# Hybrid encoder trunk on one core: the squared-ReLU units evicted wider and unscaled, one Strassen product's bank kept through all groups, PSUM divided into pairs

## The chip, the cores and the metric

The kernel runs on one core of a Trainium2 chip. The metric is the device time of one launch in microseconds: the median of three runs, with the lowest and the highest.

## The reference, cut to what matters

Two layers act on 256 tokens of width 2048. Each has three groups of attention heads with one input and one output projection, and then a squared-ReLU MLP with 8192 hidden units:

```python
def rmsnorm(x, g):
    xf = x.astype(jnp.float32)
    y = xf * lax.rsqrt(jnp.mean(xf * xf, axis=-1, keepdims=True) + EPS)
    return (y * g.astype(jnp.float32)).astype(x.dtype)
...
    for l in range(DEPTH):
        h = rmsnorm(x, norm_mix[l])
        proj = jnp.einsum('bsd,de->bse', h, w_in[l])
        ...
        mix = jnp.concatenate([rmsnorm(oa, out_gain_a[l]),
                               rmsnorm(ob, out_gain_b[l]),
                               rmsnorm(oc, out_gain_c[l])], axis=-1)
        x = x + jnp.einsum('bse,ed->bsd', mix, w_o[l])
        h = rmsnorm(x, norm_mlp[l])
        u = jax.nn.relu(jnp.einsum('bsd,df->bsf', h, w_up[l]))
        x = x + jnp.einsum('bsf,fd->bsd', u * u, w_down[l])
    return rmsnorm(x, norm_final)
```

The row factor of the MLP's norm, r = 1/sqrt(mean(x^2) + eps), is one number for each token. Since relu(r z)^2 = r^2 relu(z)^2 for r > 0, it can be applied to z, to the squared unit, or to what the down projection adds to x.

## The kernel before, in words

**Steps.** Every weight matrix streams through the core once. The work is a list of `Step`s, each with one weight tile of 512 KB. `load` (L1012) issues its DMA seven steps ahead; `split` (L1026) makes two fp32r halves of it two or three steps ahead, the high half with a cast on ScalarE (L1036, tile `whi`) and the rest with a subtraction on VectorE (L1037, tile `wlo`), three buffers of each. Then the step's `mm` runs on TensorE. Activations are held as two halves likewise, so that a product takes three matmuls: high by high, high by low, low by high.

**The background queue.** What is not a weight step (transposes, attention scores, probabilities, small sums) is a piece in a queue; `tick` after each step emits pieces whose delay is over, within a budget. That gives the order in the program. The framework then schedules each engine's instructions ahead of time by priority and readiness, so the order on an engine is fixed when the chip runs but is not the program's.

**PSUM, eight banks of 512 numbers a partition.** `score_banks` is a tile of two banks (tag S, one buffer): attention scores, and in the MLP the accumulators `a` and `d` of Strassen's products. The other six are one pool of single banks (tag `bank`), which `mm_bank` (a product's accumulator, two for each product) and `tr_bank` share: `tr_bank` serves transposes of operands (L223, L255, L271), of probabilities (L380, two banks a unit), probabilities times values (L392, L399), group sums (L443) and the row of reciprocals (L505).

**The MLP.** A layer has 32 up units q of 256 hidden columns, four steps each: z is made transposed, hidden columns on partitions, tokens in the free dimension; L675 gives 512 columns (256 of high, 256 of low activations), L680 adds the low weights. The unit's `evac` folds the two 256 column halves together in two banks (ScalarE copy L653, VectorE add L654, twice), multiplies max(z, 0) by the token's r from `rrow`, a tile with the 256 factors in every partition (L655), squares (L658), splits into halves (`u`, L660 and L661), forms Strassen's four sums S1 to S4 (`sums_of`, L696 to L698) and splits those (L700, L701). `rrow` is made by `rows` in `mlp_rs`: a diagonal of r on VectorE, a matmul by ones into a `tr_bank`, a copy. Unit 0's eviction is put off until after step (1, 0), because `rrow` is needed for it.

The down projection goes in eight groups of four units. `strassen_steps` computes 2 x 2 blocks (two token blocks, two column blocks of 512) with seven products, P1 to P7 (L806): P2 accumulates in a bank `b` of its own, P1, P6, P5 and P3 one after the other in `a`, P7 and P4 in `d`. After a product its bank is added to or subtracted from x (`evac`, L777). The first six groups have a second such set (pair 1) over half of the units for the last two column blocks; there P2 and P4 are not evicted, but `down_steps` with `shared` goes on in `b` and `d` and evicts both (L728). Groups 6 and 7 do those columns as plain products. An order written out by hand interleaves a group's Strassen steps with the next group's up steps. `layer_end` starts the next layer's operand transposes, or the final norm.

Of the kernel before, what the change touches and what calls it, by code (L numbers as in the profile page):

```python
# [23 lines left out]
P = 128  # L24
# [19 lines left out]
def tile_trunk(ctx: ExitStack, tc: tile.TileContext, x_in, xt_in, w_in, w_o, w_up, w_down,  # L44
# [57 lines left out]
    rrow = cp.tile([P, 256], F32, name="rrow")  # L102
# [99 lines left out]
    def operand_pair(key, gcol, i, src, hT):  # L202
# [8 lines left out]
        for kk in range(2):  # L211
            nc.vector.scalar_tensor_tensor(hh[:, 1, kk, :], src[kk], gs[kk], f(hh[:, 0, kk, :]),
                                           op0=ALU.mult, op1=ALU.subtract)

# [201 lines left out]
    def mix_prep(l, grp, blk, raw, mixT, sqacc, done):  # L416
# [11 lines left out]
        if first:  # L428
            acc = sp.tile([P, 256], F32, tag="sqacc", bufs=3, name=nm("sqacc"))
# [32 lines left out]
    def mode_b(banks, h_tile, wh, wl, sub, first, last, n=512, blocks=(0, 1), lo_last=False,  # L462
               by_block=False):

        def one(t, i, part):
            kk = sub[i]
            a = h_tile[i][:, int(part == "lh"), kk, t * P:(t + 1) * P]
# [17 lines left out]

    state = {}

    def layer_steps(l):
# [6 lines left out]
        def mlp_rs():  # L495
            r = rsqrt(mean_eps(st["ss2"], 4, 1.0 / D), 2)

            def rows():

                dg = mid(F32, 2, P)  # L500
                for t in range(NT):
                    nc.vector.tensor_scalar(dg[:, t, :], ident, r[:, t:t + 1], None, op0=ALU.mult)
                ps = tr_bank()
                for t in range(NT):
                    nc.tensor.matmul(ps[:, t * P:(t + 1) * P], full, dg[:, t, :], start=True, stop=True)  # L505
# [81 lines left out]
        for name in IN_CHUNKS:  # L587
# [5 lines left out]
            for k in range(nst):  # L593
# [6 lines left out]
                def mm(wh, wl, k=k, nk=nk, nst=nst, n=n, box=box, name=name):  # L600
                    if k == 0:
                        box["b"] = [mm_bank(), mm_bank()]
                    hts = [halves(st["hT"][(k * nk + i) // 2]) for i in range(nk)]
# [9 lines left out]
        for grp in OUT_ORDER:  # L613
            blks = GROUP_BLOCKS[grp]
            for j in range(4):
                box = {}
                for bi, blk in enumerate(blks):
# [6 lines left out]
                    def mm(wh, wl, grp=grp, j=j, bi=bi, blk=blk, nb=len(blks), box=box):  # L624
                        if bi == 0:
                            box["b"] = [mm_bank(), mm_bank()]
                        mode_b(box["b"], [st["mixT"][blk]] * 2, wh, wl, [0, 1], bi == 0, bi == nb - 1)
# [12 lines left out]
        uT, sT = {}, {}  # L640

        def up_steps(g):

            out_, evacs = [], []
            for q in range(4 * g, 4 * g + 4):
                box = {}

                def evac(q=q, box=box):
                    need(("rrow", l))
                    a = mid(F32, 2, 256)  # L650
                    for i in range(2):

                        nc.scalar.copy(a[:, i, :], box["b"][i][:, 256:512])  # L653
                        nc.vector.tensor_add(a[:, i, :], a[:, i, :], box["b"][i][:, 0:256])  # L654
                    nc.vector.scalar_tensor_tensor(  # L655
                        a, a, 0.0, rrow.rearrange("p (o c) -> p o c", o=1).to_broadcast([P, 2, 256]),
                        op0=ALU.max, op1=ALU.mult)
                    nc.scalar.activation(a, a, AF.Square, bias=zero1[:, 0:1])  # L658
                    u = big(F32R, 2, 2, 256)
                    nc.scalar.copy(u[:, 0], a)  # L660
                    nc.vector.tensor_sub(u[:, 1], a, f(u[:, 0]))  # L661
                    uT[q] = u
                    sums_of(q, a)

                for s in range(4):
# [3 lines left out]
                    def mm(wh, wl, s=s, q=q, box=box, evac=evac):  # L669
                        if s == 0:  # L670
                            box["b"] = [mm_bank(), mm_bank()]
                        for kk in range(4):
                            ht = st["hT2"][2 * s + kk // 2][:, kk % 2, :]
                            for fs in range(2):
                                nc.tensor.matmul(box["b"][fs], wh[:, kk, fs * P:(fs + 1) * P], ht,  # L675
                                                 start=s == 0 and kk == 0, stop=False, skip_group_check=True)
                        for kk in range(4):
                            ht = st["hT2"][2 * s + kk // 2][:, kk % 2, :]
                            for fs in range(2):
                                nc.tensor.matmul(box["b"][fs][:, 0:256], wl[:, kk, fs * P:(fs + 1) * P], ht[:, 0:256],  # L680
# [555 lines left out]
```

## Time and profile before

| | |
|---|---|
| median of 3 runs | 1995.33 us (1994.92 to 1995.36) |
| profiled execution, span | 1993.9 us, 28351 instructions |
| TensorE busy | 1980.3 us (99%), 10134 matmul records |
| VectorE, ScalarE, GpSimd busy | 1647.0, 1247.4, 396.4 us |
| HBM | 448.65 MB read, 226 GB/s over the span |
| mean granted TensorE clock | 0.999 |

The profiled execution is known by its span, from its first to its last instruction; 1.4 us lie between it and the median of the runs. A fp32 matmul of the kernel may stand as more than one record. In the profile PE is TensorE's matmuls, PEld its weight loads, DVE VectorE, ACT ScalarE, POOL GpSimd; L777 is line 777 of the kernel. A group of instructions is told as output<-inputs by the program's tile names, then shapes, count, busy time, mean ns of one, and the idle time of the engine before them with what ended it. In a timeline row the first two numbers are start and length in us, and xN merges N instructions in a row.

### The profile page before, as it was taken

Reading aid. Unit: us, or ns where it says so; the run is one execution under the profiler, and the core shown is the slowest. Engines: PE = TensorE matmul, PEld = TensorE weight load, DVE = VectorE, ACT = ScalarE, POOL = GpSimd, SP = SyncE. Lnnn points to the kernel's source line nnn. Section 1 sums busy time; section 2 is a strip of 40 time slices with the busy share of each in tenths; the row PEclk is TensorE's granted clock in tenths of the full one; section 3 lists DMA queues with packets and bytes.
Section 4 is the critical chain, followed back from the end, with each engine's and each line's share of the span. In section 5 each row is a group of like instructions: output and inputs, shape, how many; then the busy total and the mean of one; then the engine's idle time right before and its main releaser. Section 6 shows DMA issues by size and latency. Waiting matters only on the chain.

```text
span 1993.9 us, 28351 instructions
## 1 busy us (share of the span) xinstructions
PE 1980.3 (99%) x10134; PEld 1683.2 (84%) x10134; DVE 1647.0 (83%) x2197; ACT 1247.4 (63%) x1778; POOL 396.4 (20%) x462
## 2 busy tenths in 40 slices
PE   9999999999999999999999999999999999999998
PEld 7888888888888888888888888888888888888887
DVE  6777877888888888888857678778988988888887
ACT  7667756666565656566656677566666656656664
POOL 0674620001010010100008745201010001101000
PEclk9999999999999999999999999999999999999999
DMA  9755755888888888978666467568898988989884
GB/s 341 212 164 153 235 168 190 224 260 260 252 256 243 273 248 251 273 224 252 207 190 201 153 177 222 169 190 251 233 273 243 269 248 247 265 252 260 238 264 126
DMA packets 128635, 456.31 MB, mean 229 GB/s; under 512 B 14660, under 2 KB 16964, under 8 KB 128493
## 3 DMA queue, kind: packets, MB, share of 16 engines
q1 hardware_dynamic: 109052, 384.18, 56.4%
q0 software_dynamic: 19008, 69.21, 20.1%
q8 instruction: 80, 1.31, 0.3%
q10 hardware_dynamic: 432, 1.10, 0.1%
q14 instruction: 63, 0.51, 0.1%
HBM read 448.65 MB, written 2.11 MB: 226 GB/s over the span
## 4 chain that ended last, share of the span: by engine, by line
PE 96%; DVE 1%; DMA 1%; ACT 1%; issue 1%; SPq 0%; POOL 0%; POOLq 0%; DVEq 0%; ACTq 0%
PE mm L468 32%; PE mm L675 23%; PE S L806 18%; PE mm L680 12%; PE mm L806 3%; PE S L468 2%; PE tr L380 1%; PE tr L399 1%; DMA wraw<-in_w_in_dram 1%; PE S L343 1%; PE S L342 1%; PE tr L223 1%; DVE wlo L1037 0%; ACT big L360 0%; PE tr L392 0%
## 5 line engine op out<-in xcount | busy, mean ns | idle before, releaser
L1037 DVE TENSOR_TENSOR wlo<-wraw,whi 128x1024 fp32r<-128x1024 f32 (+1 forms) x517 | 634.3, 1233 | 200.9 <-ACT whi L1036 191.4
L1036 ACT CAST whi<-wraw 128x1024 fp32r<-128x1024 f32 (+1 forms) x517 | 541.2, 1051 | 360.2 <-PE mm L675 100.2
L675 PE MATMUL mm<-big,whi 128*128 128x512 f32 x2048 | 514.1, 390 | 0.0
L468 PE MATMUL mm<-whi,big 128*128 128x512 f32 (+1 forms) x1692 | 500.1, 384 | 0.8 <-ACT whi L1036 0.8
L675 PEld LDWEIGHTS mm<-big,whi 128*128 128x128 f32 x2048 | 380.5, 188 | 79.4 <-ACT whi L1036 2.2
L468 PEld LDWEIGHTS mm<-whi,big 128*128 128x128 f32 x1692 | 314.3, 188 | 61.8 <-ACT whi L1036 1.9
L680 PEld LDWEIGHTS mm<-big,wlo 128*128 128x128 f32 x2048 | 280.9, 190 | 21.2
L468 PE MATMUL mm<-wlo,big 128*128 128x512 f32 (+1 forms) x846 | 293.3, 382 | 0.0
L806 PE MATMUL S<-whi,big 128*128 128x512 f32 x1056 | 290.1, 396 | 0.0
L680 PE MATMUL mm<-big,wlo 128*128 128x256 f32 x2048 | 287.3, 282 | 0.0
L806 PEld LDWEIGHTS S<-whi,big 128*128 128x128 f32 x1056 | 184.3, 189 | 34.2 <-DVE x L777 2.8
L468 PEld LDWEIGHTS mm<-wlo,big 128*128 128x128 f32 x846 | 159.3, 188 | 28.7
L806 PE MATMUL S<-wlo,big 128*128 128x512 f32 x528 | 163.4, 391 | 0.0
L1036 ACT CAST whi<-side 128x1024 fp32r<-128x1024 f32 x88 | 92.5, 1051 | 85.3 <-PE mm L675 76.6
L1036 ACT CAST whi<-big 128x1024 fp32r<-128x1024 f32 x88 | 92.9, 1056 | 77.5 <-DVE big L788 27.7
L468 PE MATMUL mm<-spare,big 128*128 128x512 f32 (+1 forms) x606 | 140.2, 380 | 0.0
L1037 DVE TENSOR_TENSOR wlo<-side,whi 128x1024 fp32r<-128x1024 f32 x88 | 107.7, 1224 | 35.4 <-ACT whi L1036 34.6
L792 POOL DMA_DIRECT2D spare<-in_w_down_dram x44 | 38.1, 866 | 476.2 <-DVE wlo L1037 458.4
L468 PEld LDWEIGHTS mm<-spare,big 128*128 128x128 f32 x606 | 108.9, 188 | 20.4
L1037 DVE TENSOR_TENSOR wlo<-big,whi 128x1024 fp32r<-128x1024 f32 x88 | 107.7, 1224 | 21.5 <-ACT whi L1036 21.3
L792 POOL DMA_DIRECT2D side<-in_w_down_dram x44 | 38.3, 881 | 400.9 <-DVE mid L654 150.8
L806 PEld LDWEIGHTS S<-wlo,big 128*128 128x128 f32 x528 | 99.2, 188 | 22.2
(163 smaller groups left out, 2310.3 us busy)
## 6 DMA issues: line engine op xcount, KB each, us to landing
wraw<-in_w_up_dram SPq DMA_DIRECT2D x256, 512.0 KB, 4.8
wraw<-in_w_down_dram SPq DMA_DIRECT2D x124, 512.0 KB, 5.1
wraw<-in_w_in_dram SPq DMA_DIRECT2D x119, 512.0 KB, 3.7
side<-in_w_down_dram SPq DMA_DIRECT2D x88, 512.0 KB, 5.2
wraw<-in_w_o_dram SPq DMA_DIRECT2D x64, 512.0 KB, 3.7
side<-in_w_down_dram POOLq DMA_DIRECT2D x44, 512.0 KB, 7.5
spare<-in_w_down_dram SPq DMA_DIRECT2D x44, 512.0 KB, 5.9
spare<-in_w_down_dram POOLq DMA_DIRECT2D x44, 512.0 KB, 5.5
```

The costliest lines, as they stand in the source:

```text
L223: nc.tensor.transpose(psv[:, kk, t, :], x[:, t, c0:c0 + P], ident)
L342: nc.tensor.matmul(o, st, u.kh[:, kh, :], start=True, stop=False)
L343: nc.tensor.matmul(o, st, u.kl[:, kh, :], start=False, stop=True)
L380: nc.tensor.transpose(ps[:, c * P:(c + 1) * P], u.p[:, s, kb * P:(kb + 1) * P], ident)
L399: nc.tensor.matmul(ps, u.V[:, kb, u.kv, :, :], pt[:, kb, :], start=n == 0, stop=n == 3)
L468: nc.tensor.matmul(banks[t][:, 0:n], a, (wl if part == "hl" else wh)[:, i, :], start=first and i == 0 and part == "hh", stop=last and i == ...
L675: nc.tensor.matmul(box["b"][fs], wh[:, kk, fs * P:(fs + 1) * P], ht, start=s == 0 and kk == 0, stop=False, skip_group_check=True)
L680: nc.tensor.matmul(box["b"][fs][:, 0:256], wl[:, kk, fs * P:(fs + 1) * P], ht[:, 0:256], start=False, stop=s == 3 and kk == 3, skip_group_ ...
L792: nc.gpsimd.dma_start(tile, src(par, j, h).rearrange("p (k n) -> p k n", k=2), accum_op=ALU.add)
L806: nc.tensor.matmul(o, ops[i][a], w[:, i, :], skip_group_check=True, start=fresh and h == 0 and i == 0 and a == 0 and w is wh, stop=h == ti ...
L1036: last_act[0] = nc.scalar.copy(h[:, part], w[:, part]).ins
L1037: last_lo[0] = nc.vector.tensor_sub(lo[:, part], w[:, part], f(h[:, part])).ins
```

## The change

- `evac` of an up unit works on both banks at once: one copy, one add, Relu and Square on ScalarE, in a tile `wide` (8 x 128 columns, one buffer) that takes the four blocks and, from `sums_of`, the four sums; then one cast and one subtraction make both halves of up to all eight. No factor r is applied.
- r^2 (the power -1 of the mean square) and its negative are kept per token in `rsq`, and `residual` applies them where a product is added to x. `rows`, `rrow` and the putting off of unit 0 go.
- P2's bank is kept: it starts at group 0 and goes on accumulating. In the first pair it is evicted only after group 7, in the second only after the shared product of group 5.
- The six banks become two `pair` tiles of two banks (`mm_pair`, for products) and two single banks (`tr`, for all that `tr_bank` serves and for the two kept banks).
- The group sums of the attention outputs use the `wide` tile.

```diff
+    def four_k():
+        return sp.tile([P, 8, P], F32, tag="wide", bufs=1, name=nm("wide"))
...
-    def mm_bank():
-        return pp.tile([P, 512], F32, tag="bank", bufs=6, name=nm("mm"))
+    def mm_pair():
+        return pp.tile([P, 2, 512], F32, tag="pair", bufs=2, name=nm("mm"))
+    def mm_banks():
+        two = mm_pair()
+        return [two[:, 0, :], two[:, 1, :]]
     def tr_bank():
-        return pp.tile([P, 512], F32, tag="bank", bufs=6, name=nm("tr"))
+        return pp.tile([P, 512], F32, tag="tr", bufs=2, name=nm("tr"))
...
+    def residual(xs, bank, l, t, sign=1):
+        nc.vector.scalar_tensor_tensor(xs, bank, rsq[:, l, int(sign < 0), t:t + 1], xs, op0=ALU.mult, op1=ALU.add)
...
         def mlp_rs():
-            r = rsqrt(mean_eps(st["ss2"], 4, 1.0 / D), 2)
-            def rows():
-                dg = mid(F32, 2, P)
-                for t in range(NT):
-                    nc.vector.tensor_scalar(dg[:, t, :], ident, r[:, t:t + 1], None, op0=ALU.mult)
-                ps = tr_bank()
-                for t in range(NT):
-                    nc.tensor.matmul(ps[:, t * P:(t + 1) * P], full, dg[:, t, :], start=True, stop=True)
-                nc.vector.tensor_copy(rrow, ps[:, 0:256])
-                flags.add(("rrow", l))
-            add(rows, 0.45, delay=D_R, front=True)
+            ms = mean_eps(st["ss2"], 4, 1.0 / D)
+            nc.gpsimd.tensor_tensor(rsq[:, l, 0], ms, mone[:, 0:2], op=ALU.pow)
+            nc.gpsimd.tensor_scalar(rsq[:, l, 1], rsq[:, l, 0], -1.0, None, op0=ALU.mult)
...
                 def evac(q=q, box=box):
-                    need(("rrow", l))
-                    a = mid(F32, 2, 256)
-                    for i in range(2):
-                        nc.scalar.copy(a[:, i, :], box["b"][i][:, 256:512])
-                        nc.vector.tensor_add(a[:, i, :], a[:, i, :], box["b"][i][:, 0:256])
-                    nc.vector.scalar_tensor_tensor(
-                        a, a, 0.0, rrow.rearrange("p (o c) -> p o c", o=1).to_broadcast([P, 2, 256]),
-                        op0=ALU.max, op1=ALU.mult)
-                    nc.scalar.activation(a, a, AF.Square, bias=zero1[:, 0:1])
-                    u = big(F32R, 2, 2, 256)
-                    nc.scalar.copy(u[:, 0], a)
-                    nc.vector.tensor_sub(u[:, 1], a, f(u[:, 0]))
-                    uT[q] = u
-                    sums_of(q, a)
+                    au = four_k()
+                    a = au[:, 4:8, :].rearrange("p (k t) c -> p k (t c)", k=2)
+                    nc.scalar.copy(a, box["b"][:, :, 256:512])
+                    nc.vector.tensor_add(a, a, box["b"][:, :, 0:256])
+                    nc.scalar.activation(a, a, AF.Relu, bias=zero1[:, 0:1])
+                    nc.scalar.activation(au[:, 0:4, :].rearrange("p (k t) c -> p k t c", k=2)[:, :, ::-1, :],
+                                         a.rearrange("p k (t c) -> p k t c", t=2), AF.Square, bias=zero1[:, 0:1])
+                    sums_of(au)
+                    n0 = int(g < 6 and q % 4 < 2)
+                    uh, ul = big(F32R, 8, P), big(F32R, 8, P)
+                    nc.scalar.copy(uh[:, n0:8], au[:, n0:8])
+                    nc.vector.tensor_sub(ul[:, n0:8], au[:, n0:8], f(uh[:, n0:8]))
+                    uT[q] = uh, ul
...
-        def sums_of(q, a):
-            v = a.rearrange("p k (t c) -> p (k t) c", t=2)
-            sm = mid(F32, 4, P)
...
+        def sums_of(au):
+            nc.vector.tensor_sub(au[:, 4:6, :], au[:, 1:3, :], au[:, 0:1, :].to_broadcast([P, 2, P]))
+            nc.vector.scalar_tensor_tensor(au[:, 6, :], au[:, 5, :], -1.0, au[:, 1, :], op0=ALU.mult, op1=ALU.subtract)
+            nc.vector.scalar_tensor_tensor(au[:, 7, :], au[:, 6, :], -1.0, au[:, 3, :], op0=ALU.mult, op1=ALU.subtract)
...
                     def evac(t):
                         xs = x[:, t, j * 512:(j + 1) * 512]
-                        nc.vector.tensor_add(xs, xs, box["b"][t])
+                        residual(xs, box["b"][t], l, t)
...
-                    evac(0)
+                    if not shared or gs == (5,):
+                        evac(0)
                     evac(1)
...
             def evac(bank, t, j, sign):
                 xs = x[:, t, 1024 * pair + j * 512:1024 * pair + (j + 1) * 512]
-                op = nc.vector.tensor_add if sign > 0 else nc.vector.tensor_sub
-                op(xs, xs, bank)
+                residual(xs, bank, l, t, sign)
...
                         if (name, h) == ("P2", 0):
-                            box["b"] = mm_bank()
+                            if pair not in keep:
+                                keep[pair] = tr_bank()
+                            box["b"] = keep[pair]
...
-                                                 start=fresh and h == 0 and i == 0 and a == 0 and w is wh,
+                                                 start=fresh and h == 0 and i == 0 and a == 0 and w is wh and (bk != "b" or g == 0),
...
-                        if h == tiles[-1] and not (pair and name in ("P2", "P4")):
+                        if h == tiles[-1] and not (pair and name == "P4") and not (name == "P2" and (pair or g < 7)):
                             evac(o, *dst)
```

More of the change, by code (lines that the diff above doesn't have):

```diff
@@ L101, in tile_trunk @@
     nc.vector.memset(full, 1.0)
-    rrow = cp.tile([P, 256], F32, name="rrow")
+    rsq = cp.tile([P, L, 2, NT], F32, name="rsq")
     mhalf = cp.tile([P, 16], F32, name="mhalf")
@@ L428, in mix_prep @@
         if first:
-            acc = sp.tile([P, 256], F32, tag="sqacc", bufs=3, name=nm("sqacc"))
+            if not sqacc:
+                sqacc["all"] = four_k()
+            n = 2 * "ACB".index(grp)
+            acc = sqacc["all"][:, n:n + 2, :].rearrange("p a c -> p (a c)")
             sqacc[grp] = acc
@@ L484, in mode_b, with of @@
                     one(t, i, part)
+    def of(h):
+        return lambda part, kk, t: h[:, part, kk, t * P:(t + 1) * P]
     state = {}
@@ L601, in mm @@
                     if k == 0:
-                        box["b"] = [mm_bank(), mm_bank()]
-                    hts = [halves(st["hT"][(k * nk + i) // 2]) for i in range(nk)]
+                        box["b"] = mm_banks()
+                    hts = [of(halves(st["hT"][(k * nk + i) // 2])) for i in range(nk)]
                     mode_b(box["b"], hts, wh, wl, [(k * nk + i) % 2 for i in range(nk)], k == 0, k == nst - 1, n,
@@ L637, in layer_steps @@
                     steps.append(Step(src, 2, 512, pre, mm))
-        uT, sT = {}, {}
+        uT, keep = {}, {}
         def up_steps(g):
-            out_, evacs = [], []
+            out_ = []
             for q in range(4 * g, 4 * g + 4):
```

43 lines of the change are left out of this document (15 added, 28 removed).

## The prediction

> **What bounds the kernel now.** I read the page's busy times first, then the table by stages, the waits, the groups by shape, and the timeline where the change touches the order.
>
> ```profile
> PE 1980.3 (99%) x10134; PEld 1683.2 (84%) x10134; DVE 1647.0 (83%) x2197; ACT 1247.4 (63%) x1778; POOL 396.4 (20%) x462
> ```
>
> TensorE is busy for 1980.3 of 1993.9 us. By stages (columns: stretch, length, then busy time of PE, PEld, DVE, ACT, POOL, granted clock, DMA share, GB/s):
>
> ```profile
> 199.00:315.00 116.00, 114.86 (x586) 96.97 (x585) 93.53 (x147) 73.92 (x138) 43.55 (x49) 1.00 0.65 196
> 315.00:1000.00 685.00, 685.00 (x3503) 582.82 (x3502) 590.90 (x744) 422.63 (x520) 56.03 (x65) 1.00 0.83 246
> 1190.00:1306.00 116.00, 114.85 (x588) 97.09 (x587) 92.58 (x147) 74.09 (x139) 43.48 (x49) 1.00 0.64 195
> 1960.00:1994.00 34.00, 25.93 (x136) 22.00 (x134) 23.17 (x36) 14.72 (x22) 1.12 (x2) 0.93 0.26 94
> ```
>
> In the first layer's MLP (315 to 1000) PE never stops, though DVE is busy 86% of the time; the stage of attention and output projection loses 1.1 us in each layer, the tail 8.1 us. So work taken from DVE or ACT is worth only what PE waits for them. Those waits:
>
> ```profile
> ACT whi L1036 <- PE mm L675: 210.0, 182, 2.1
> ...
> PEld S L806 <- DVE x L777: 2.8, 15, 0.3
> PEld S L806 <- DVE x L728: 2.7, 10, 0.4
> ```
>
> ACT waits 210 us for PE to free weight buffers: the weight splits run ahead of PE, and that is the cover for all that the change does to ACT and DVE. PE's loader waits only 5.5 us for evictions.
>
> **The change part by part.** The rows that price it:
>
> ```profile
> L1037 DVE TENSOR_TENSOR wlo<-wraw,whi 128x1024 fp32r<-128x1024 f32 x515 | 633.0, 1235 | 200.9 <-ACT whi L1036 191.4 <-issue 7.9 <-PE tr L223 0.4
> L1036 ACT CAST whi<-wraw 128x1024 fp32r<-128x1024 f32 x515 | 540.0, 1052 | 360.2 <-PE mm L675 100.2 <-PE S L806 96.4 <-PE mm L468 75.0
> ...
> L777 DVE TENSOR_TENSOR x<-x,S 128x512 f32<-128x512 f32 x156 | 106.5, 683 | 1.3 <-PE S L806 1.1
> ...
> L654 DVE TENSOR_TENSOR mid<-mid,mm 128x256 f32<-128x256 f32 x128 | 47.8, 415 | 0.7
> L658 ACT ACTIVATE mid<-mid,zero 128x512 f32<-128x512 f32 x64 | 46.2, 722 | 15.2 <-DVE mid L655 15.2
> L655 DVE SCALAR_TENSOR_TENSOR mid<-mid,rrow 128x512 f32<-128x512 f32 x64 | 44.0, 687 | 0.7
> L701 DVE TENSOR_TENSOR big<-mid,big 128x512 fp32r<-128x512 f32 x64 | 43.9, 686 | 0.0
> L661 DVE TENSOR_TENSOR big<-mid,big 128x512 fp32r<-128x512 f32 x64 | 43.8, 685 | 0.0
> ...
> L653 ACT COPY mid<-mm 128x256 f32<-128x256 f32 x128 | 41.0, 371 | 24.6 <-PE mm L680 24.6
> L660 ACT CAST big<-mid 128x512 fp32r<-128x512 f32 x64 | 39.7, 620 | 1.7
> L700 ACT CAST big<-mid 128x512 fp32r<-128x512 f32 x64 | 39.5, 617 | 19.6 <-DVE mid L698 19.5
> ...
> L381 ACT CAST big<-tr 128x512 fp32r<-128x512 f32 x64 | 34.4, 590 | 0.6
> L633 DVE SCALAR_TENSOR_TENSOR x<-mm,sm,x 128x512 f32<-128x512 f32 x48 | 33.9, 744 | 0.2
> ...
> L696 DVE TENSOR_TENSOR mid<-mid 128x256 f32<-128x256 f32 x64 | 26.8, 419 | 0.0
> ...
> L697 DVE SCALAR_TENSOR_TENSOR mid<-mid,mid 128x128 f32<-128x128 f32 x64 | 18.4, 287 | 0.4
> L698 DVE SCALAR_TENSOR_TENSOR mid<-mid,mid 128x128 f32<-128x128 f32 x64 | 18.4, 287 | 0.3
> ...
> L505 PE MATMUL tr<-mid,full 128*128 128x128 f32 x8 | 1.2, 273 | 0.0
> ```
>
> (1) An up unit's eviction, 64 times. DVE before: 2 x 415 + 687 + 685 + 419 + 2 x 287 + 686 = 3.88 us. After: one add of 512 columns (683), the same sums (419 + 2 x 287), one subtraction of up to 1024 columns (1235) = 2.91 us; 62 us less in all. ACT before: 2 x 371 + 722 + 620 + 617 = 2.70 us; after: a copy of 512 from PSUM (590), Relu and Square (722 each), a cast of 1024 (1052) = 3.09 us, 25 us more. On the path I cost both at nothing: DVE and ACT stay ahead of PE. Without that cover the chain to a usable uT, longer by about 2 us (casts and subtraction of 1024 instead of 512, and the sums ahead of them), would count only where Strassen's P1 follows its unit directly, at the first group of each layer (later groups have two steps of the shared product between). Bounds 0 and 2 x 2 us; I take 0.3, since other ready matmuls can go first there.
>
> (2) Evictions to x. By the loops there are 233; P2 keeps its bank in 7 groups and the shared product's first half in 5, in each layer: 24 fewer, 16.4 us of DVE. The other 209 become scalar_tensor_tensor, 744 instead of 683 ns: 12.7 us back. On the path: the L728 waits are 10 in number, as are the starts of a group whose S banks wait behind a pair of evictions of which the first now goes (five a layer). One of them, and an undisturbed product after it:
>
> ```profile
> 446.35 1.75 PE L675 MATMUL mm<-big,whi 128*128 128x512 f32 x7
> 448.05 1.20 PE L806 MATMUL S<-whi,big 128*128 128x512 f32 x4
> ...
> 450.71 1.09 PE L806 MATMUL S<-whi,big 128*128 128x512 f32 x4
> ```
>
> Seven matmuls at 0.229 us would end their turn at 447.95, the product starts 0.10 later, and its four take 0.11 longer: 0.2 us, ten times, 2.2 us given to the change (bounds: nothing and the 5.5 us of both waits). Against it stands 0.061 us where PE waits on an eviction directly, and twice in the tail: +0.3 (bounds 0 and 3, if each reuse of Strassen's first bank paid it).
>
> (3) The row of reciprocals (L502 to L506): 8 PE records, 1.2 us busy with overlap, disappear from PE's stream: -1.0 us (0.9 to 1.2). In exchange POOL gets one tiny multiplication per layer. No DMA is added or moved, so SP's and POOL's transfers keep their order.
>
> (4) PSUM. Before, six banks served products and transposes together; now products have two pairs, and transposes, probabilities times values and small sums have two banks. Pairs are no problem: a product takes at least two steps and its eviction follows at once, so the pair before last is free. In the MLP no tr tile is made between the operand transposes and the last group, so holding both banks costs nothing there. Attention is the place. A tile's bank is held from its first PE instruction to its last DVE read:
>
> ```profile
> 90.65 1.03 PE L380 MATMUL tr<-ident,big 128*128 128x128 f32 x8
> ...
> 146.53 1.04 PE L255 MATMUL tr<-ident,big 128*128 128x128 f32 x8
> ...
> 150.19 1.03 PE L380 MATMUL tr<-ident,big 128*128 128x128 f32 x8
> ...
> 212.29 0.33 PE L255 MATMUL tr<-ident,big 128*128 128x128 f32 x1 [1.14 <-ACT big L517]
> ...
> 478.73 0.51 PE L680 MATMUL mm<-big,wlo 128*128 128x256 f32 x3
> 479.07 1.16 PE L806 MATMUL S<-whi,big 128*128 128x512 f32 x4
> ...
> 1296.23 1.03 PE L223 MATMUL tr<-ident,x 128*128 128x128 f32 x8
> ```
> ```profile
> 92.21 0.84 DVE L412 TENSOR_TENSOR mid<-tr,ot 64x256 f32<-64x256 f32 x2
> ...
> 154.02 2.82 DVE L262 SCALAR_TENSOR_TENSOR big<-tr,big 64x512 fp32r<-64x512 f32 x4 [3.52 <-ACT big L259]
> ...
> 478.29 0.68 DVE L777 TENSOR_TENSOR x<-x,S 128x512 f32<-128x512 f32 x1
> ...
> 1295.87 0.87 DVE L212 SCALAR_TENSOR_TENSOR big<-tr,gn,big 128x256 fp32r<-128x256 f32 x2
> ```
>
> At 146.53 two tiles are written; DVE has read the first by 154.02 + 1.41 = 155.4. At 150.2 the next two are begun, into banks that will no longer exist: the first would wait 5.2 us. Done so for 152 tiles, 42 start with two or more unread (the first in the 90.65 row, its second tile, until 93.05; the last at 1296.66, 0.07 us). Kept in today's order and shifted by what was waited already, the waits sum to 57.8 us: the upper bound. The lower is zero, since PE's order is a list schedule in which ready matmuls pass waiting ones: at 478 to 479 the product that had to wait for an eviction (ends 478.97) starts at 479.07, in the middle of an up step, at a loss of 0.1 us. Where the schedule misjudged the other engines it cost 1.14 us (212.29). I take a wait up to one projection step as bridged (the 12 matmuls of the row below, 2.75 us, 0.229 each) and the rest of longer ones as paid: per layer 5.22, 3.62 and 3.19 are longer, the rest is 2.47 + 0.87 + 0.44 = 3.8, so +7.6 us for two layers.
>
> ```profile
> 76.61 2.75 PE mm L468 x12
> ```
>
> The Trainium skill (Trainium Kernel Development and Optimization, Best Practices) says that consistent bubbles can mean that SBUF or PSUM ran out. By that every one of the 42 would leave a bubble; at the 212.29 row's 1.14 us each this part would be 48 us, an estimate, against 7.6 by the rows.
>
> **The sum**: 0.3 - 2.2 + 0.3 - 1.0 + 7.6 = +5.0 us on the span of 1993.9. The median of the runs, 1995.33, stands 1.4 above that span, so 2000.3 us.
>
> **The rivals.** *All bridged* (transfer of waits hidden anyway): the D_T, D_PV and similar delays leave room, and PE always has a projection step to run. Against it: ACT and DVE in attention run in a fixed order and stood still in cross waits, as 212.29 shows. 1995.3 - 2.6 = 1992.7 us, within 0.2%. *Faster*: with 66 us taken from DVE, all 5.5 us of eviction waits go, and the evacuations ahead of the query transposes come early enough for the 1.14 us in both layers: -1.0 - 5.5 - 2.3 = 1986.5 us; it decides from 4.0 us on and only if no bank wait is paid. *Order kept*: if PE cannot pass the waiting transposes, -2.6 + 57.8, so 2050 us; the 479.07 row speaks against it. *Clock*: the granted clock is 1.00 in the stages with a 1.1 us stop and 0.93 in the last 34 us, which hold 8.1 us of idle: 2.4 us lost. If the three long waits of each layer are paid in full (24.1 us) and the four longest each cost such a loss (9.5), 1995.3 - 2.6 + 33.6 = 2026 us. The Trainium skill (TensorE: Matmul & The Clock Gate, Part 1) has the clock halved after an idle window of about 3.4 us; by that the loss would be some 4 x 1.7 = 6.8 us instead of 9.5, an estimate. No run here shows a stop of that length inside the kernel.
>
> **How the numbers follow.** Partly bridged 0.42 (own range 1996 to 2012; 0.10 of it under 1999.3), all bridged 0.33 (0.04 of it below 1991.3), faster 0.13, order kept 0.07, clock 0.05. About 0.2% (4.0 us) is what a measurement here can tell from no change. Faster 0.13 + 0.04 = 0.17; same 0.10 + 0.29 = 0.39; slower 0.32 + 0.07 + 0.05 = 0.44. The range 1990.5 to 2016 leaves out order kept, clock and most of the faster case, about 0.2.
>
> **What would show it.** Right: PE's waits on tr tiles with a DVE or ACT releaser in 60 to 290 and 1050 to 1280, a few us per layer; PE below full in those stages and still full in the MLP; the L728 waits for S gone; DVE near 1580 us, ACT near 1270. Wrong: no tr waits in attention (then all bridged), clock below 1.00 there, or MLP stretches in which PE waits for the new eviction's chain or for its single wide buffer.

## The result and the profile after

| | before | after |
|---|---|---|
| median | 1995.34 us (1994.92 to 1995.58, 4 runs) | 2007.65 us (2006.50 to 2008.09, 4 runs) |
| ratio to before | | 1.0059 [1.0045, 1.0073] |
| profiled span | 1993.9 us | 2005.4 us |
| mean granted clock | 0.999 | 0.999 |

The change makes the kernel 12.3 us slower. That is the sign that was forecast and lies in the range of 1990.5 to 2016 us, but it is more than twice the 5.0 us of the sum. The busy row of the page of after:

```profile
PE 1986.2 (99%) x10126; PEld 1680.8 (84%) x10126; DVE 1603.6 (80%) x1975; ACT 1276.6 (64%) x1714; POOL 402.1 (20%) x464
```

VectorE has 43 us less to do, TensorE eight records fewer, and yet TensorE is "busy" 6 us longer. The ends of matmuls are modelled in this profile, so its busy time says little here; how long each stage lasts says more. The marks are the first `mm<-big,whi` matmul of a layer's first up unit and the last record of that layer's MLP in a Strassen product; each number is the distance between two such starts or ends in the trace (us):

| kernel | start to MLP 0 | MLP 0 | to MLP 1 | MLP 1 | end | span |
|---|---|---|---|---|---|---|
| before | 315.7 | 671.4 | 319.0 | 668.5 | 19.3 | 1993.9 |
| after | 321.8 | 670.9 | 323.7 | 669.1 | 19.9 | 2005.4 |
| two `tr` banks alone (e2) | 323.2 | 671.6 | 324.9 | 668.6 | 20.0 | 2008.3 |
| three `tr` banks alone (e5) | 319.7 | 672.8 | 320.3 | 671.1 | 19.3 | 2003.2 |
| kept bank alone (e3) | 315.6 | 671.4 | 318.9 | 670.0 | 19.3 | 1995.2 |
| row scaling alone (e10) | 315.1 | 669.6 | 319.0 | 667.8 | 18.6 | 1990.1 |
| new eviction alone (e4) | 314.7 | 669.7 | 319.1 | 667.8 | 18.6 | 1989.9 |
| after, six single banks (e1) | 316.3 | 669.7 | 319.1 | 667.9 | 18.6 | 1991.6 |

After against before: +6.1 and +4.7 in the two stages ahead of the MLPs, +0.1 in the two MLPs together, +0.6 at the end. TensorE's loader now waits like this (line waited for, us in total, times, longest):

```profile
PEld S L803 <- DVE x L225: 9.4, 35, 0.6
PEld tr L392 <- issue: 6.5, 14, 0.6
PEld tr L283 <- DVE big L394: 2.7, 2, 1.4
PEld tr L392 <- POOL big L383: 2.5, 2, 1.3
PEld tr L267 <- DVE avs L156: 2.0, 1, 2.0
```

L392 (L380 before) transposes probabilities, L283 and L267 operands: the `tr` tiles, with VectorE reads (L394, L156) as releasers. No wait on a `tr` tile is longer than 2.0 us. In the timeline (start, length, then idle time before it):

```profile
35.53 0.67 DVE L156 COPY avs<-tr 8x512 f32<-8x512 f32 x1
...
36.26 0.66 PE L267 MATMUL tr<-ident,big 128*128 128x128 f32 x4 [1.76 <-DVE avs L156]
```
```profile
157.65 1.84 POOL L383 TENSOR_SCALAR big<-big,sm 128x256 f32<-128x256 f32 x4
...
159.10 0.63 PE L392 MATMUL tr<-ident,big 128*128 128x128 f32 x4 [0.87 <-POOL big L383]
```

The first is a plain bank wait: the one-time product at L154 (`avp`) sits in a `tr` bank until VectorE has copied it. The second is by its releaser no bank wait: the transposes wait for probabilities that GpSimd is still scaling. The granted clock stays at 1.00 in both attention stages, and fewer matmuls fit into the same stretch (first row before, then the two of after; columns as in the prediction's table):

```profile
60.00:290.00 230.00, 228.86 (x1166) 193.51 (x1165) 179.23 (x268) 154.39 (x295) 139.88 (x160) 1.00 0.62 183
```
```profile
60.00:290.00 230.00, 226.82 (x1146) 188.59 (x1145) 176.51 (x271) 153.44 (x298) 138.62 (x159) 1.00 0.61 181
...
1050.00:1280.00 230.00, 226.77 (x1147) 188.63 (x1146) 174.16 (x268) 152.57 (x296) 137.28 (x157) 1.00 0.61 182
```

The waits of before list nothing on GpSimd at this line: there the same scaling (L371) ends at 155.94 and its transposes begin at 156.52, so nothing waits. With two banks the transposes stand in TensorE's order ahead of the scaling's end.

### The profile page after: what moved, and what is told of

It is laid out like the page before. It is cut to its first block, busy times and chain, and to the rows that moved or that the text cites. A ratio compares the mean times of both kernels' runs of the same rounds, so it can differ in the third digit from the quotient of the medians.

```text
span 2005.4 us, 28100 instructions
## 1 busy us (share of the span) xinstructions
PE 1986.2 (99%) x10126; PEld 1680.8 (84%) x10126; DVE 1603.6 (80%) x1975; ACT 1276.6 (64%) x1714; POOL 402.1 (20%) x464
## 4 chain that ended last, share of the span: by engine, by line
PE 62%; DVE 1%; ACT 1%; issue 0%; POOL 0%; POOLq 0%; DVEq 0%; ACTq 0%
PE mm L483 18%; PE mm L682 16%; PE S L803 13%; PE mm L687 8%; PE tr L803 2%; PE tr L483 1%; PE S L483 1%; PE tr L392 1%; PE tr L411 0%; PE tr L235 0%; PE S L354 0%; PE S L355 0%; DVE wlo L1034 0%; PE tr L404 0%; PE tr L267 0%
## 5 line engine op out<-in xcount | busy, mean ns | idle before, releaser
L1034 DVE TENSOR_TENSOR wlo<-wraw,whi 128x1024 fp32r<-128x1024 f32 (+1 forms) x517 | 634.1, 1233 | 220.8 <-ACT whi L1033 218.2
L483 PE MATMUL mm<-whi,big 128*128 128x512 f32 (+1 forms) x1596 | 471.7, 386 | 1.2 <-DVE x L225 0.7
L483 PEld LDWEIGHTS mm<-whi,big 128*128 128x128 f32 x1596 | 296.0, 189 | 57.7 <-ACT whi L1033 1.5
L483 PE MATMUL mm<-wlo,big 128*128 128x512 f32 (+1 forms) x798 | 279.6, 383 | 0.0
L483 PEld LDWEIGHTS mm<-wlo,big 128*128 128x128 f32 x798 | 150.5, 189 | 27.3 <-DVE wlo L1034 0.2
L1034 DVE TENSOR_TENSOR wlo<-side,whi 128x1024 fp32r<-128x1024 f32 x88 | 107.6, 1223 | 46.3 <-ACT whi L1033 46.2
L225 DVE SCALAR_TENSOR_TENSOR x<-S,rsq,x 128x512 f32<-128x512 f32 x168 | 125.5, 747 | 4.6 <-PE S L803 2.6
L1034 DVE TENSOR_TENSOR wlo<-big,whi 128x1024 fp32r<-128x1024 f32 x88 | 107.4, 1220 | 16.8 <-ACT whi L1033 16.7
```

Of the source, the lines that this page charges most:

```text
L225: nc.vector.scalar_tensor_tensor(xs, bank, rsq[:, l, int(sign < 0), t:t + 1], xs, op0=ALU.mult, op1=ALU.add)
L483: nc.tensor.matmul(banks[t][:, 0:n], a, (wl if part == "hl" else wh)[:, i, :], start=first and i == 0 and part == "hh", stop=last and i == ...
L1034: last_lo[0] = nc.vector.tensor_sub(lo[:, part], w[:, part], f(h[:, part])).ins
```

## The experiments

The theory to test: the loss is the split of the PSUM banks, and there the two that transposes share. Rivals: the new eviction (one wide buffer, a longer chain), or the kept bank that holds one of the two.

**e1: after with one pool of six single banks**, and so the copy and the add of an up unit bank by bank.

```diff
-        return pp.tile([P, 512], F32, tag="tr", bufs=2, name=nm("tr"))
+        return pp.tile([P, 512], F32, tag="bank", bufs=6, name=nm("tr"))
...
-        two = mm_pair()
-        return [two[:, 0, :], two[:, 1, :]]
+        return [pp.tile([P, 512], F32, tag="bank", bufs=6, name=nm("mm")) for _ in range(2)]
```

> The changed kernel with PSUM as before: one pool of six single banks for products and transposes, so an up unit's eviction has two copies and two adds of 256 columns instead of one of 512; the kept banks and the residual scaling stay. Bank theory (transposes have too few banks in attention): the 12 us go away, 1993 to 1996 us, and PE's waits on transposes fall back to those of the kernel before. Eviction theory (the longer chain, the single wide buffer, dearer residual additions): it stays within 3 us of the changed kernel, 2004 to 2008. Kept-bank theory (two banks fewer for the up units now hurt): slower than the changed kernel, over 2008.

Measured: 1992.84 us, 0.9986 [0.9977, 0.9995]. The whole loss is gone, and the kernel is 2.6 us faster than before. (The bank theory had 1993 to 1996.) On `tr` tiles its loader waits for the same two things as before's (3.6 us in 4 waits, 2.0 in 2) and no longer for L388, the transposes of probabilities:

```profile
PEld S L800 <- DVE x L221: 5.7, 23, 0.3
PEld tr L263 <- ACT big L522: 3.6, 4, 1.6
PEld tr L263 <- ACT big L572: 2.0, 2, 1.6
```

Against e1, after is longer by 5.5, 1.2, 4.6, 1.2 and 1.3 us in the five stages.

**e2: before with two `tr` banks** and four for products; the bank of P2 and that of the warm-up come from the two, as in after. Nothing else is changed.

```diff
     def mm_bank():
-        return pp.tile([P, 512], F32, tag="bank", bufs=6, name=nm("mm"))
+        return pp.tile([P, 512], F32, tag="bank", bufs=4, name=nm("mm"))
     def tr_bank():
-        return pp.tile([P, 512], F32, tag="bank", bufs=6, name=nm("tr"))
+        return pp.tile([P, 512], F32, tag="tr", bufs=2, name=nm("tr"))
```

> The kernel before with one thing changed: transposes, probabilities times values, small sums and Strassen's bank b get a pool of two single banks, products one of four. Bank theory: 2004 to 2008 us, with 4 to 5 us more lost on PE in each attention stage and 1 to 2 us in the first 60 us. Eviction and kept-bank theories: 1995 to 1997, as before.

Measured: 2009.6 us, 1.0072 [1.0057, 1.0087]. This edit alone makes a loss as large as the whole change, and more than the 2004 to 2008 expected: +7.5 and +5.9 us in the stages ahead of the MLPs, 0.3 in the two MLPs together. The waits of its loader have the pattern of after, and the timeline shows one of them in full:

```profile
PEld tr L380 <- issue: 6.4, 14, 0.7
PEld tr L380 <- POOL big L371: 4.4, 2, 2.2
```
```profile
158.00 0.39 PE L468 MATMUL mm<-wlo,big 128*128 128x512 f32 x1
160.16 0.63 PE L380 MATMUL tr<-ident,big 128*128 128x128 f32 x4 [1.78 <-POOL big L371]
160.55 0.71 PE L468 MATMUL mm<-whi,big 128*128 128x512 f32 x2
```

TensorE stands in the middle of a projection step, which goes on right behind the transposes. The projection shows no wait of its own; it stands behind the transposes in an order that was fixed when the program was scheduled, and here TensorE does not pass what is late. GpSimd's scaling (L371) runs at 158.71 in e2 and at 154.10 in before, 4.6 us earlier: what the transposes wait for comes later as well.

**e3: before with only the kept bank.**

```diff
-                    evac(0)
+                    if not shared or gs == (5,):
+                        evac(0)
...
-                            box["b"] = mm_bank()
+                            if pair not in keep:
+                                keep[pair] = mm_bank()
+                            box["b"] = keep[pair]
```

> The kernel before with only P2's bank kept through the groups (24 evictions fewer, plain additions at x, six shared banks of which two are held in the MLP). Bank theory: no loss; the waits of PE's loader for the S banks at a group's start fall, 1993 to 1995.5 us. Kept-bank theory: four banks for the up units are too few, over 1999.

Measured: 1996.61 us, 1.0006 [0.9997, 1.0016]. Neither a cost nor a gain that can be measured: the 2.2 us forecast are not there, and 1993 to 1995.5 was missed. All ten of the waits that should have gone are still there, and longer in total (2.7 us in before):

```profile
PEld S L809 <- DVE x L728: 3.6, 10, 0.4
```

The start of a group that the prediction showed at 446 to 450 us:

```profile
446.29 1.07 PE L675 MATMUL mm<-big,whi 128*128 128x512 f32 x4
...
446.56 0.68 DVE L728 TENSOR_TENSOR x<-x,S 128x512 f32<-128x512 f32 x1
...
447.29 0.77 PEld L809 LDWEIGHTS S<-whi,big 128*128 128x128 f32 x4 [0.36 <-DVE x L728]
447.30 1.21 PE L809 MATMUL S<-whi,big 128*128 128x512 f32 x4
```

The first eviction is gone, the second comes earlier, and the schedule puts the product three matmuls earlier (after four of L675 instead of seven), where it waits for the same eviction again. The second MLP is 1.5 us longer in the profiled run (670.0 against 668.5); over all runs the interval holds no change.

**e4: before with only the new eviction and the scaling at the residual** (`wide` tile, wide split, `residual`), six single banks, no kept bank. The edit is the `four_k`, `residual`, `mlp_rs`, `evac` and `sums_of` parts of the diff, with the copy and the add of a unit bank by bank.

> The kernel before with only the new eviction and the scaling at the residual (no kept bank, six single banks, two copies and two adds of 256). Bank theory: 1993 to 1996.5 us, with the row of reciprocals worth 1 us and residual additions of 0.745 instead of 0.683 us worth up to 1.5 us the other way. Eviction theory: 2003 to 2008.

Measured: 1992.24 us, 0.9984 [0.9975, 0.9994]. Alone, this part is a gain, and this kernel beats both before and after.

**e10: before with only the scaling moved**: the row of reciprocals is gone, and with it the putting off of unit 0; the unit's eviction stays in its old narrow pieces.

```diff
-                    nc.vector.scalar_tensor_tensor(
-                        a, a, 0.0, rrow.rearrange("p (o c) -> p o c", o=1).to_broadcast([P, 2, 256]),
-                        op0=ALU.max, op1=ALU.mult)
+                    nc.vector.tensor_scalar(a, a, 0.0, None, op0=ALU.max)
...
-                op = nc.vector.tensor_add if sign > 0 else nc.vector.tensor_sub
-                op(xs, xs, bank)
+                residual(xs, bank, l, t, sign)
```

> The kernel before with only the scaling moved to the residual and the row of reciprocals gone; the unit's eviction stays bank by bank, in 256 column pieces, with its two separate splits. Theory of the forecast (the row is worth 1.0 us, dearer residual additions 0.3, the wide splits nothing): 1994.0 to 1995.0 us. Rival (most of the 3.1 us that the new eviction gave in the kernel before comes with the row: eight records out of TensorE's stream and unit 0 no longer put off): 1992 to 1993 us. Second rival (it comes from the wide splits, the row is nothing): 1995 us or more.

Measured: 1992.13 us, 0.9981 [0.9972, 0.9990]. The first rival held: as fast as e4 within the interval. So the fewer, wider operations are worth nothing that can be measured; all of the gain comes with the moved scaling and what goes with it. Before and e10 around the row (L505 is its matmul; up step L680 to L680 and L671 to L671):

```profile
324.05 1.11 PE L680 MATMUL mm<-big,wlo 128*128 128x256 f32 x8
325.00 0.60 PE L505 MATMUL tr<-mid,full 128*128 128x128 f32 x4
325.37 2.09 PE L675 MATMUL mm<-big,whi 128*128 128x512 f32 x8
327.30 1.11 PE L680 MATMUL mm<-big,wlo 128*128 128x256 f32 x8
```
```profile
323.47 1.12 PE L671 MATMUL mm<-big,wlo 128*128 128x256 f32 x8
324.42 2.00 PE L666 MATMUL mm<-big,whi 128*128 128x512 f32 x8
326.26 1.12 PE L671 MATMUL mm<-big,wlo 128*128 128x256 f32 x8
```

3.25 against 2.79 us: the row costs 0.46 us in the first layer, and 0.9 in all if the second is like it. The MLPs of e10 are shorter by 1.8 and 0.7 us, so 1.6 more have gone there. Waits for evictions to x are one candidate: before had 25 of 5.5 us, e10 has the first line below. But e4, whose MLPs are as short as e10's, has the second, so the waits of the loader alone do not account for the 1.6 us:

```profile
PEld S L793 <- DVE x L217: 2.9, 11, 0.3
```
```profile
PEld S L797 <- DVE x L221: 5.6, 23, 0.3
```

At the place of e3's rows the timeline of e10 shows:

```profile
445.19 1.75 PE L666 MATMUL mm<-big,whi 128*128 128x512 f32 x7
...
445.99 0.75 DVE L217 SCALAR_TENSOR_TENSOR x<-S,rsq,x 128x512 f32<-128x512 f32 x1
...
446.79 1.20 PE L793 MATMUL S<-whi,big 128*128 128x512 f32 x4
```

Seven matmuls at 0.229 us end their turn at 446.79, and the product starts at 446.79: the 0.10 us that it waited in before is gone, with both evictions still there. The VectorE operation that replaces the multiplication by the row is shorter (group rows: 423 ns in e10; the 687 of L655 stands in the prediction), and so the same pair of evictions can end earlier against TensorE. That this is the cause is read from the rows of this one place; it was not tried by itself, and neither was unit 0's earlier eviction. Of the span's 3.8 us the rest is 0.7 in the tail (below) and 0.6 ahead of the first MLP, where nothing was traced to a cause.

**e5: before with three banks for transposes** and three for products.

```diff
-        return pp.tile([P, 512], F32, tag="bank", bufs=6, name=nm("tr"))
+        return pp.tile([P, 512], F32, tag="tr", bufs=3, name=nm("tr"))
```

> The kernel before with three single banks for the transposes' side and three for products (instead of two and four in the run with two). Bank-count theory: the third bank takes most of the loss away, each attention stage loses 2.5 to 4 us on PE instead of 8.3 and the first 60 us are as before (5.3); in the MLP three banks for an up unit's two may cost up to 5 us of their own, so the total is left open, 1996 to 2004. Rival, that it is the split of the pool as such (a product can no longer take a bank that a transpose frees): the attention stages stay at 7 us or more.

Measured: 2005.32 us, 1.0048 [1.0030, 1.0066]. That is above the 1996 to 2004 expected. But the second attention stage is down to 320.3 us (319.0 before, 324.9 with two banks), and from 60 to 290 us TensorE is busy for 228.65 us, against 228.86 in before and 225.38 in e2: in attention a third bank buys back most of the loss, though products have a bank less than in e2.

```profile
PEld mm L675 <- DVE x L728: 3.6, 12, 0.3
PEld tr L380 <- issue: 2.6, 4, 1.1
PEld mm L675 <- DVE mid L654: 2.1, 6, 0.4
```

Now the products are short of a bank: waits on `mm` tiles (L675) appear, and the MLPs are 1.4 and 2.6 us longer than before. The 4.0 us that the stage ahead of the first MLP still loses (319.7 against 315.7) lie mostly in its first 60 us, where TensorE gets through 271 records (288 in before): at 30.8 us a projection stands for 1.87 us behind ScalarE (L567), which before does not have, and the granted clock is 0.91 from 20 to 40 us (1.00 in before): by that figure some 1.8 us are lost to a slower clock, an estimate. Six banks in one pool serve both stages at different times; no fixed split of the six that was tried does.

**e6: after with a smaller budget of background work behind each step.**

```diff
-    LOOK_LOAD, LOOK_SPLIT, LOOK_PREP, LOOK_T2, LOOK_T3, BUDGET = 7, 2, 5, 7, 8, 2.2
+    LOOK_LOAD, LOOK_SPLIT, LOOK_PREP, LOOK_T2, LOOK_T3, BUDGET = 7, 2, 5, 7, 8, 1.0
```

> The changed kernel with the background queue's budget for one tick at 1.0 instead of 2.2, so that a unit's transposes (two banks) and another unit's products with the values (one bank) are no longer emitted behind the same weight step. Theory that the collisions come from pieces emitted together: attention stages at 3 to 5 us instead of 6.9 and 7.1, 1999 to 2004 us in all. Rival, that the order of the pieces does not matter because the schedule's estimates of the other engines are what is off: 6 to 9 us, within 2 us of the changed kernel, or slower if attention's last pieces come late.

Measured: 2014.92 us, 1.0095 [1.0079, 1.0111]. Not the 1999 to 2004 us of the theory, though its collisions did become fewer: the waits ahead of L392 without a releaser are 1.6 us in 4, against 6.5 in 14 in after. What the smaller budget costs is more than that: the last pieces come late, as the waits of the group sums show (L458, twice a stop of TensorE of 2.48 us), and the stages ahead of the MLPs take 323.4 and 327.5 us.

```profile
PEld tr L458 <- POOL big L562: 5.7, 2, 2.9
```

Behind the second of these stops, which ends at 1130.16, the granted clock is 0.91 from 1120 to 1140 us, so part of the loss is a slower clock.

**e7: after with other banks for three tiles**: the one-time product in half of the score tile, the two half-products at the very end in the two single banks.

```diff
-            avp = tr_bank()
+            avp = score_banks().rearrange("p (b i) n -> p b (i n)", i=2)[:, 0]
...
-                        tail = mm_banks()
+                        tail = [tr_bank(), tr_bank()]
```

> The changed kernel with two tiles moved: the T5 vector's matmul in the first 60 us uses a bank of the score tile, and the two last column halves of the final product use the two single banks instead of the two halves of one pair. Theory that these two places pay for the banks too: the 1.9 us wait of the second query transposes for that vector's copy goes (first 60 us at 5 to 6 us), and the 0.9 us wait of the last half product for the eviction of the other half goes, 2004.5 to 2006 us. Rival, that the time is only moved on: 2007 to 2008.

Measured: 2004.73 us, 1.0045 [1.0030, 1.0060], as expected. The start is 2.5 us shorter than in after (319.3 to the first MLP) and the end 1.0 (18.9). The end of after shows why:

```profile
1994.36 0.48 DVE L225 SCALAR_TENSOR_TENSOR x<-mm,rsq,x 128x256 f32<-128x256 f32 x1
...
1994.89 0.39 PE L483 MATMUL mm<-whi,big 128*128 128x256 f32 x1 [0.73 <-DVE x L225]
```

The second half-product writes the second bank of a pair while VectorE still reads the first. They share no element, yet TensorE waits until the read is over: a pair is guarded as one tile.

**e8: after with the copy and the add of a unit bank by bank**, on the same pair tile.

```diff
-                    nc.scalar.copy(a, box["b"][:, :, 256:512])
-                    nc.vector.tensor_add(a, a, box["b"][:, :, 0:256])
+                    for i in range(2):
+                        nc.scalar.copy(a[:, i, :], box["b"][:, i, 256:512])
+                        nc.vector.tensor_add(a[:, i, :], a[:, i, :], box["b"][:, i, 0:256])
```

> The changed kernel with the eviction's copy and add done bank by bank again (256 columns, twice each), all else as changed. Theory that the wide add on VectorE delays Strassen's evictions: PE's loader waits for the S banks fall from 9.4 to about 5.7 us and the MLP stages lose 3.7 and 3.6 us instead of 4.9 and 4.8, 2005 to 2006 us. Rival, that the pairs as such or the two held banks do it: waits and time unchanged, 2007 to 2008.

Measured: 2022.53 us, 1.0134 [1.0118, 1.0150], far from both ranges. The MLPs take 678.4 and 676.6 us instead of 670.9 and 669.1. e1 and e4 run the same narrow pieces on single banks at no cost, so it is the pair. Its waits:

```profile
PEld S L804 <- ACT whi L1034: 12.1, 12, 1.1
ACT wide L661 <- DVE wide L662: 10.8, 8, 1.3
ACT wide L663 <- DVE wide L662: 10.7, 24, 0.5
```

ScalarE's second copy (L661) stands behind VectorE's first add (L662), a wait that e1 does not list; the weight split on ScalarE (L1034) comes later for it, and Strassen's product waits for that split. So the wide form does matter, but only because of the pair: it avoids a cost that the new PSUM layout made.

**e9: after with the moves of e7, and a unit's transposed probabilities in one pair tile**, evicted by one copy and one subtraction.

```diff
+        two = mm_pair()
         for kb in range(2):
-            ps = tr_bank()
...
-                nc.tensor.transpose(ps[:, c * P:(c + 1) * P], u.p[:, s, kb * P:(kb + 1) * P], ident)
+                nc.tensor.transpose(two[:, kb, c * P:(c + 1) * P], u.p[:, s, kb * P:(kb + 1) * P], ident)
-            nc.scalar.copy(u.ph[:, kb, :], ps)
-            nc.vector.tensor_sub(u.pl[:, kb, :], ps, f(u.ph[:, kb, :]))
+        nc.scalar.copy(u.ph, two)
+        nc.vector.tensor_sub(u.pl, two, f(u.ph))
```

> The kernel after with three moves that leave the number of banks as it is: the transposed probabilities of a unit go to one pair tile (one 1024 column copy and one subtraction instead of two of 512 each), a unit's probabilities times values go to half of the score tile in the first group as in the run before, the two half-products at the end go to the two single banks. Theory (the two single banks are too few for transposes, wherever the relief comes from): the two attention stages lose 3 to 4.5 us each instead of 7, the end nothing, so 1997 to 2001 us. Rival (a pair is held as one tile, and projections need the pairs too): the products wait for the pair instead, the attention stages stay at 6 us or more, 2004 us or slower.

Measured: 2003.11 us, 1.0037 [1.0024, 1.0051]. The rival's mechanism held, though its 2004 us were missed by 0.9: against e7 the stage ahead of the first MLP goes from 319.3 to 320.0 us and the one ahead of the second from 323.7 to 323.0 only, and now the products wait:

```profile
PEld mm L483 <- DVE big L394: 3.1, 6, 0.6
PEld mm L392 <- issue: 3.0, 4, 0.9
```

## Why the prediction was right or wrong

The measured sum, by kernels run alone: two `tr` banks +14.2 us (e2, 2009.6 less 1995.42, the median of before beside these runs), the scaling with the new eviction -3.2 (e4), the kept bank +1.2 (e3, whose interval holds no change). Together 12.2, and the change measured +12.3. That the sum meets it to 0.1 us is partly luck: e2 has single banks for products where after has pairs, its stages ahead of the MLPs lose more than after's (7.5 and 5.9 us against 6.1 and 4.7), and it has nothing of what the pairs cost elsewhere. Against e1, which differs from after in the banks and the narrow copy and add that go with them, the loss is 14.8 us.

**Banks (+7.6): the cause was right, the rule that priced it was not.** This is the step that failed, by a factor of nearly two (14.2 in e2). The rule was that TensorE bridges a wait up to one projection step and pays the rest of the longer ones. The long waits, of 5.2, 3.6 and 3.2 us a layer, never came: the largest that any `tr` tile shows in after is 2.0 us, which by the rule would have cost nothing, being shorter than a step of 2.75. So the range holds because it was wide, not because of this rule. In place of the long waits stand many small ones: fourteen of up to 0.6 us ahead of L392 (the profile names no releaser for them, and e1 does not have them), two of 1.4 where operand transposes (L283) wait for a bank, two of 1.3 where moved transposes meet GpSimd's late scaling. The list of 42 was worked out in today's order, and the waits that are paid belong to the new order. Two places were missing from the sum: the one-time product at 35.5 us (1.8) and the end, where a pair is one tile (0.7); e7 removed both. "Pairs are no problem" was wrong for these half-products. The MLPs of after are also 1.2 us longer than those of e1, with more waits for evictions to x (9.4 us in 35 against 5.7 in 23). In e2 and e3 there are 25 such waits (5.4 and 6.6 us), as in before, so it is the pairs, the wide copy and add on them, or the kept banks together with them; which of these was not tried.

**Kept bank (-2.2): not there.** The waits did not vanish with the eviction that they waited for; at the place shown for e3 the product was moved forward until it waited again, and the other nine waits are still there too. And a loader's wait is not lost time one for one: e1 has 5.7 us of them on x and e10 2.9, and their MLPs are equal to 0.1 us.

**The row (-1.0): right**, 0.9 by the rows of e10. That the sum of all but the banks came out as forecast (-2.6, measured -2.0 from e4 and e3) is so by another split of it.

**The eviction at the first group (+0.3) and the dearer residual (+0.3): not seen; the tail went the other way.** I had counted twice 0.061 us against the change there; e10's end is 0.7 us shorter. In before the last eviction starts 0.78 us after its matmul's end (1985.93), in e10 0.04 (1982.78):

```profile
1985.05 0.88 PE L468 MATMUL mm<-spare,big 128*128 128x256 f32 x6
...
1986.11 0.43 DVE L744 TENSOR_TENSOR x<-x,big 128x256 f32<-128x256 f32 x1 [0.77 <-ACT mid L917]
...
1986.63 0.15 DVE L925 TENSOR_SCALAR sm<-sm 128x1 f32<-128x1 f32 x1
1986.71 0.41 DVE L741 TENSOR_TENSOR x<-x,mm 128x256 f32<-128x256 f32 x1
```
```profile
1981.90 0.88 PE L472 MATMUL mm<-spare,big 128*128 128x256 f32 x6
...
1982.20 0.42 DVE L732 TENSOR_TENSOR x<-x,big 128x256 f32<-128x256 f32 x1
...
1982.72 0.15 DVE L912 TENSOR_SCALAR sm<-sm 128x1 f32<-128x1 f32 x1
1982.82 0.48 DVE L217 SCALAR_TENSOR_TENSOR x<-mm,rsq,x 128x256 f32<-128x256 f32 x1
```

In both the eviction is queued behind an addition and the small sums of the other half (L744 to L925, L732 to L912). In before that addition waits 0.77 us for ScalarE and starts only after the matmuls' end; in e10 it starts 0.58 us ahead of it. Why ScalarE is earlier there was not traced.

**The rivals.** *All bridged* and *faster* fell with e2. *Order kept* was far off, as the row at 479.07 had said. *Clock*: in after no wait on a `tr` tile is longer than 2.0 us and the granted clock stays at 1.00, so its condition was not met. Two other runs did meet it, behind stops of 1.87 (e5) and 2.48 us (e6), while an equal stop in e6's first layer, ending at 132.57, left the clock at 1.00. Its price of 2.4 us was read from the wrong place: in before the clock is 1.00 from 1960 to 1986 us and 0.70 from 1986 on, where TensorE has no matmul left to lose time with. The Trainium skill's rule on consistent bubbles (Trainium Kernel Development and Optimization, Best Practices), which the prediction had weighed at 48 us, pointed to the right cause: the bubbles are there and PSUM ran out. The price was too high, since a bubble is worth 0.5 us in the largest group (6.5 us in 14), not 1.14.

**What would show it.** Right: `tr` waits in the two attention stages, MLPs full, ScalarE at 1276.6. Wrong: the waits of S did not go (9.4 us, 35 times), and VectorE stands at 1603.6 instead of 1580, since my sum added whole durations where neighbours overlap (L741 above starts 0.08 us after L925, which takes 0.15). Added up so, VectorE's instructions did become shorter by 74 us (1774.2 to 1700.0), but its busy time by only 43.

## What to carry to other kernels

When one pool of PSUM banks is split by use, price it at the stage with the most small tiles, and test the split alone before anything is built on it: here it cost 14.2 us and hid a gain of 3.2. Here TensorE was full and its order fixed ahead, and the missing banks did not show as one long wait but as many stops of about half a microsecond, some with a releaser that has nothing to do with the bank. And of a change with several parts, run each by itself: moving the row factor to the residual, in the old layout, is the version to keep (0.9981 of before), and the wide evictions added nothing to it that could be measured.

## What the runs showed of the hardware and had not been expected

- Two banks of one tile do not give two engines independent access under this framework, though they touch different banks: 0.73 us at the end of after, and some 7.5 us in each MLP in e8 (678.4 against 670.9, 676.6 against 669.1).
- In e5 the granted clock is 0.91 from 20 to 40 us, around a stop of TensorE of 1.87 us. In e6 it is 0.91 from 1120 to 1140 us, around one of two stops of 2.48 us; around the other, from 120 to 140 us, it is 1.00. The stops of 1.76 us in after and 1.78 us in e2 left it at 1.00. What decides between them was not tried.
- Less work on VectorE gave nothing where it is not the bound: e10 and e4 take 1992.13 and 1992.24 us, with VectorE busy for 1640.3 us in the first and 1622.9 in the second. The busy rows of e10 and of e4:

```profile
PE 1977.7 (99%) x10126; PEld 1682.9 (85%) x10126; DVE 1640.3 (82%) x2191; ACT 1246.1 (63%) x1778; POOL 398.8 (20%) x464
```
```profile
PE 1977.8 (99%) x10126; PEld 1682.3 (85%) x10126; DVE 1622.9 (82%) x2063; ACT 1280.5 (64%) x1778; POOL 398.1 (20%) x464
```
